# A decoder trunk's causal attention: heads kept in the rows of their product, and the causal mask as a VectorE add

## The chip, the core and the metric

One core of a Trainium2 chip runs the whole kernel in one launch. The metric is the device time of one execution in microseconds (us), as a median of several executions. A core has a matrix engine (TensorE, PE in the profile, with its weight loads as PEld), three other compute engines (VectorE = DVE, ScalarE = ACT, GpSimd = POOL), each with its own queue of instructions that it works off in order, and SyncE (SP), whose queue starts the transfers (DMAs). Matrix products land in PSUM, a small memory of banks; VectorE and ScalarE can read and write it, and everything else lies in SBUF, 128 partitions (rows) wide.

## What is computed

A trunk of two layers over 512 tokens of width 1024. In each layer four branches read the same input: RWKV-7 time mixing, multi-head latent attention, a convolution module and cross-attention into 256 memory tokens. Each branch is gated, projected and merged; an output product and a layer norm follow. The change is in the attention with latents (8 heads, 64 plain and 32 rotary channels each):

```python
q = (_rms_norm(q_lat, q_norm) @ w_uq).reshape(B, S, H, MLA_NOPE + MLA_ROPE)
kv = (_rms_norm(kv_lat, kv_norm) @ w_ukv).reshape(B, S, H, MLA_NOPE + MLA_V)
...
q_full = jnp.concatenate([q_nope, q_pe], axis=-1)
k_full = jnp.concatenate(
    [k_nope, jnp.broadcast_to(k_pe[:, :, None, :], (B, S, H, MLA_ROPE))], axis=-1)
...
s = jnp.einsum('bqhd,bkhd->bhqk', q_blk, k).astype(jnp.float32) * scale
s = jnp.where(key_idx[None, :] <= q_idx[:, None], s, MASK_VALUE)
pr = jax.nn.softmax(s, axis=-1).astype(v.dtype)
return jnp.einsum('bhqk,bkhd->bqhd', pr, v)
```

It is computed for blocks of 128 queries. Products are kept close to f32 precision: each operand is split into a high part in f32r (a shorter f32 for which TensorE is fast) and a low part, the rest, also in f32r.

## The kernel before

**A plan orders everything.** The program is written out while it is planned. Class `Plan` (line 67) keeps a clock for each engine and adds an estimated cost with each instruction; every branch is a generator that yields where something else may go first. `Plan.run` (147) steps the task that is due, or else takes the next piece of the stream of items (`stream`, 1860), which hold the large projections and serve as filler for TensorE. What results is a fixed order of instructions on each engine; no engine reorders its instructions at run time beyond that. All matrix products go through helper `MM` (line 286 of the profile), transposes through `TR` (291), vector and scalar work through `Engine` (235) and DMAs through `DMA` (298), so the profile shows these lines, and groups are told apart by the names of their tiles. All DMAs are issued from SP's one queue.

**Items and weights.** `stream` takes items in their listed order, skipping those that are not ready (`pick`, 1866). An item's weights are loaded as raw f32 (two buffers, `WR`), and split by ScalarE (high part) and VectorE (low part). A product of an item lands in one of the two banks of pool `pp`; the next one can use a bank when the instructions that read it are done.

**A product of split operands** is three matmuls (`mm3`, 467): high x low, high x high, low x high. 

**Pairs of heads.** `pair_item` (1416) computes queries ("pq") and keys ("pk") of two heads at once, 64 channels each, so that head 0 is on rows 0 to 63 of the product and head 1 on rows 64 to 127. `heads` (1441) splits the whole product into a high and a low tile ("xqh", "xql", "xkh", "xkl"), and eight DMAs for a pair copy the halves to rows 0 to 63 of each head's own tiles ("qT", "qTl", "kTh", "kTl"). The 32 rotary channels come to rows 64 to 95 by DMAs from "qrh", "qrl" (queries, in `pair_item`) and "krh", "krl" (keys, in `key_rotary`, 1299). The scores thus contract over 96 rows.

**Blocks.** `pair` (1454) spawns one `mla_block` (1471) for each head and each block of 128 queries, 64 in all over both layers, with up to three under way. A block is a chain across three engines: scores into a bank "ms" (three matmuls over 128 to 512 columns), the mask, row maximum on VectorE ("nmm"), exponential with row sum on ScalarE ("mP"), reciprocal and scaling on VectorE ("mP"), transposes on TensorE ("mt"), a copy on ScalarE ("mPT"), and for every two blocks of both heads the product with the values ("mo", 64 columns of weights). The mask is a fourth matmul into the diagonal 128 columns of "ms": the identity in bf16 as weights ("idb") times a tile with 0 and -1e30 ("causal").

**Around it.** The cross-attention ("xs", "xt", "xo") and the convolution run beside the causal attention. The convolution is 4 x 31 taps per layer on VectorE ("cacc", `taps`, 1123), each a pass over 128 x 512; after each it yields "slack", which lets the plan put it off until VectorE's clock. Its norm begins with transposes "ct". `mix` (682) makes the token shift of the RWKV branch in two passes: ScalarE scales the product, shifted by one column, into a tile "tsh", and VectorE adds the scaled product.

## Time and profile before

| | us |
|---|---|
| median of 3 executions | 1520.82 |
| lowest and highest | 1518.16, 1522.56 |
| the profiled execution, device time | 1519.87 |
| its span, first to last instruction | 1518.1 |
| first and last score matmul of layer 0 (from the span's start) | 121.5 and 223 |
| the same of layer 1 | 903 and 983 |

How to read the views: a window row gives a stretch of the span and for each engine its busy time and count of instructions. A wait row names the waiting engine and tile, after "<-" what ended the wait, then the sum in us, how many times, and the longest. A timeline row gives the start, the duration in us, the engine, line, operation, the tiles (out <- in), the shape and the count of merged instructions, and in brackets the idle time of the engine before it and what ended that. A group row ends with the busy time, the mean in ns of one, and the idle time before them. A matmul's duration covers its way through the array; matmuls overlap, so what one costs is read from the distance of the starts.

### The profile page before, as it was taken

What the parts mean: (1) busy time and instruction counts of PE and PEld (TensorE: products, weight loads), DVE (VectorE), ACT (ScalarE), POOL (GpSimd) and SP (SyncE); (2) the same over time, 40 slices, a digit from 0 to 9 for tenths busy, and PEclk for the clock granted to TensorE, in tenths of its full rate; (3) what the DMA queues carried; (4) which work ended last, traced back from release to release, by engine and by line L of the source; (5) the groups of instructions that cost most, each with busy time, mean ns of one, the idle gap of its engine ahead of it and who ended that gap; (6) DMA issues with size and microseconds to landing.
All of it is one profiled execution on the core that took longest, in us unless ns stands there. A gap on an engine that the chain in (4) does not pass through costs nothing.

```text
span 1518.1 us, 29700 instructions
## 1 busy us (share of the span) xinstructions
PE 1485.7 (98%) x11896; PEld 1238.0 (82%) x11896; DVE 1072.7 (71%) x2231; ACT 686.6 (45%) x1499; POOL 135.8 (9%) x323
## 2 busy tenths in 40 slices
PE   8999999999999999999999999999999999999997
PEld 8877788887887878888999877888887878788886
DVE  5788988765757675555554889997766586756747
ACT  5535653445245453344255556533443545443432
POOL 0000000030402021000010000000030303120002
PEclk9999999999999999999999999999999999999999
DMA  6443333322232323433343252433232323235231
GB/s 211 124 113 93 104 100 98 98 85 83 74 93 60 94 74 93 139 98 114 123 146 114 81 125 69 121 107 97 81 99 61 93 64 93 69 95 181 98 116 65
DMA packets 89018, 153.54 MB, mean 101 GB/s; under 512 B 41008, under 2 KB 47152, under 8 KB 88880
## 3 DMA queue, kind: packets, MB, share of 16 engines
q1 hardware_dynamic: 88880, 151.65, 33.9%
q8 instruction: 93, 1.52, 0.4%
q14 instruction: 45, 0.37, 0.1%
HBM read 134.32 MB, written 5.77 MB: 92 GB/s over the span
## 4 chain that ended last, share of the span: by engine, by line
PE 89%; DVE 5%; DMA 2%; ACT 2%; issue 1%; SPq 1%; POOL 0%; ACTq 0%; DVEq 0%; POOLq 0%
PE ps_m L286 22%; PE po L286 11%; PE ps_cg L286 3%; PE ps_rg L286 3%; PE ps_v L286 3%; PE ps_xg L286 3%; PE ps_mg L286 3%; PE ps_k L286 3%; PE ps_r L286 3%; PE ps_val L286 3%; PE pz L286 2%; PE ms L286 2%; PE pl L286 2%; PE ps_glu L286 2%; PE ps_xq L286 2%; PE x L286 2%
## 5 line engine op out<-in xcount | busy, mean ns | idle before, releaser
L235 DVE SCALAR_TENSOR_TENSOR cacc<-hpad,prm,cacc 128x512 f32<-128x512 f32 x240 | 178.9, 748 | 3.3
L235 ACT ACTIVATE tm<-ps_m,prm 128x512 f32<-128x512 f32 x64 | 44.1, 689 | 148.5 <-PE ps_m L286 134.7
L235 DVE SCALAR_TENSOR_TENSOR mt<-tm,po 128x512 f32<-128x512 f32 x48 | 33.0, 687 | 79.2 <-PE po L286 79.1
L235 POOL TENSOR_SCALAR ZT<-W 64x256 f32<-64x256 f32 x8 | 4.8, 600 | 621.8 <-DMA W<-scr 287.7
L235 POOL TENSOR_TENSOR ZT<-ZT,tmpW 64x14 f32<-64x14 f32 (+6 forms) x112 | 44.0, 393 | 8.8
L235 ACT ACTIVATE mP<-ms,nmm 128x512 f32<-128x512 f32 (+3 forms) x64 | 33.7, 529 | 18.3 <-DVE nmm L235 17.4
L235 POOL TENSOR_TENSOR tmpW<-ZT,W 64x14 f32<-64x14 f32 (+6 forms) x112 | 39.9, 356 | 7.9
L235 ACT COPY mPT<-mt 128x512 f32<-128x512 f32 (+3 forms) x64 | 26.7, 429 | 22.4 <-PE mt L291 17.1
L235 DVE TENSOR_TENSOR merged<-merged,mt 128x512 f32<-128x512 f32 x48 | 33.8, 704 | 1.6
L235 DVE TENSOR_REDUCE nmm<-ms 128x1 f32<-128x512 f32 (+3 forms) x64 | 29.9, 483 | 0.6 <-PE ms L286 0.2
L235 POOL TENSOR_SCALAR gr<-gm 128x8 f32<-128x8 f32 x8 | 2.3, 286 | 311.2 <-DVE gm L235 311.2
L291 PE MATMUL mt<-cst,mP 128*128 128x128 f32 x160 | 27.1, 276 | 2.6 <-DVE mP L235 2.2
L235 DVE SCALAR_TENSOR_TENSOR merged<-tm,po 128x512 f32<-128x512 f32 x16 | 11.0, 687 | 22.0 <-PE po L286 20.3
L235 DVE TENSOR_SCALAR mP<-mP,smm 128x512 f32<-128x512 f32 (+3 forms) x64 | 24.8, 387 | 2.3
L235 ACT ACTIVATE yb<-yb,mr,gr 128x64 f32<-128x64 f32 x64 | 22.1, 430 | 9.0 <-DVE mr L235 9.0
L235 POOL TENSOR_SCALAR lrs<-lmv 128x1 f32<-128x1 f32 x8 | 2.5, 315 | 263.5 <-DVE lmv L235 261.8
L291 PEld LDWEIGHTS mt<-cst,mP 128*128 128x128 f32 x160 | 18.6, 141 | 8.2 <-ACT mo L235 2.2
L235 ACT ACTIVATE z<-z,lnb,lrs 128x256 f32<-128x256 f32 (+1 forms) x16 | 9.6, 647 | 31.2 <-DVE lnb L235 31.2
L286 PE MATMUL ms<-kTl,qT 96*128 96x512 f32 (+3 forms) x64 | 22.2, 347 | 0.0
L286 PE MATMUL mo<-mPT,v 128*64 128x128 f32 x320 | 21.4, 278 | 0.5 <-ACT mPT L235 0.5
L286 PE MATMUL ms<-kTh,qT 96*128 96x512 f32 (+3 forms) x64 | 20.6, 322 | 0.0
L286 PEld LDWEIGHTS mo<-mPT,v 128*64 128x64 f32 x320 | 17.3, 136 | 4.0 <-issue 2.9
(3535 smaller groups left out, 5323.2 us busy)
## 6 DMA issues: line engine op xcount, KB each, us to landing
w<-in_w_ch_dram SPq DMA_DIRECT2D x146, 512.0 KB, 3.6
w<-in_w_o_dram SPq DMA_DIRECT2D x32, 512.0 KB, 3.6
w<-in_w_out_dram SPq DMA_DIRECT2D x16, 512.0 KB, 3.6
w<-in_w_lat_dram SPq DMA_DIRECT2D x16, 336.0 KB, 3.3
w<-in_w_mk_dram SPq DMA_DIRECT2D x8, 512.0 KB, 3.5
w<-in_w_mv_dram SPq DMA_DIRECT2D x8, 512.0 KB, 3.5
w<-in_w_qk_dram SPq DMA_DIRECT2D x8, 320.0 KB, 3.1
x<-in_xT_dram SPq DMA_DIRECT2D x8, 256.0 KB, 5.6
```

The source lines that it names most:

```text
L235: return self.plan.keep(f(*a, **k))
L286: plan.keep(nc.tensor.matmul(o, lhsT, rhs, start=start, stop=stop))
L291: plan.keep(nc.tensor.transpose(o, i, ident))
```

## The change

Heads keep the rows on which their product lands. Tiles of queries and keys get 128 rows. Head 0 of a pair has its plain channels on rows 0 to 63 and its rotary part on 64 to 95, as before, and contracts over rows 0 to 95. Head 1 has its plain channels on rows 64 to 127, its rotary part on rows 32 to 63 and zeros, set by GpSimd, on rows 0 to 31, and contracts over all 128. So `heads` splits each half of the product straight into the head's tiles, two instructions on ScalarE and two on VectorE in place of one and one, and the eight DMAs of a pair go. The mask matmul goes too; VectorE adds the tile "causal" to the diagonal 128 columns in PSUM ahead of the maximum.

Three changes of the order go with it: pair items are marked "apart" and are not picked right behind each other if another item is ready; taps yield "idle" and are due one step behind VectorE's clock; and `mix` no longer needs "tsh". With "idb" and "tsh" gone, the pool of general tiles has 33 slots, and one tile of the convolution moves to another pool.

```diff
-U_SLOTS = 32
+U_SLOTS = 33
...
-                elif task[2] == "slack":
-                    task[0] = max(task[0], self.clk["DVE"])
+                elif task[2] in ("slack", "idle"):
+                    task[0] = max(task[0], self.clk["DVE"] + (task[2] == "idle"))
...
         def mix(i, ps, dst):
-            S.activation(tsh[:, 1:512], ps[:, 0:511], AF.Copy, scale=pr("mu", i))
-            V.scalar_tensor_tensor(out=dst, in0=ps, scalar=PRM[l][2][:, i:i + 1], in1=tsh, op0=ALU.mult, op1=ALU.add)
+            S.activation(dst, ps, AF.Copy, scale=PRM[l][2][:, i:i + 1])
+            V.scalar_tensor_tensor(out=dst[:, 1:512], in0=ps[:, 0:511], scalar=pr("mu", i), in1=dst[:, 1:512], op0=ALU.mult, op1=ALU.add)
...
                 L["taps"][i] = k
-                yield "slack"
+                yield "idle"
...
-                t, z = u(f"ctn{i}" + t_), u(f"yc{i}" + t_)
+                t, z = sp.tile([128, 512], F32, tag="tg", name=f"ctn{i}" + t_), u(f"yc{i}" + t_)
...
-                    L["kT"] = [tuple(m(f"kT{n}{i}" + t_, 512, f"kT{n}{i}", 1, 96, F32R) for n in "hl") for i in range(4)]
+                    L["kT"] = [tuple(m(f"kT{n}{i}" + t_, 512, f"kT{n}{i}", 1, 128, F32R) for n in "hl") for i in range(4)]
+                    for i in (1, 3):
+                        for x in L["kT"][i]:
+                            G.memset(x[0:32].bitcast(F32), 0.0)
...
-            for kT in L["kT"]:
+            for i, kT in enumerate(L["kT"]):
                 for x, y in zip(kT, kr):
-                    DMA(x[64:96].bitcast(F32), y.bitcast(F32))
+                    DMA(x[ROPE[i % 2]].bitcast(F32), y.bitcast(F32))
...
+        ROPE, ROWS = [slice(64, 96), slice(32, 64)], [slice(0, 96), slice(0, 128)]
...
                     for x, y in zip(qT[h], qpe[hh // 2]):
-                        DMA(x[64:96].bitcast(F32), y[r:r + 32].bitcast(F32), f"qTpe{hh}{h}" + t_)
+                        if h:
+                            G.memset(x[0:32].bitcast(F32), 0.0)
+                        DMA(x[ROPE[h]].bitcast(F32), y[r:r + 32].bitcast(F32), f"qTpe{hh}{h}" + t_)
...
-        def heads(T, ps, n, s, there):
-
-            parts = [u(f"x{n}{x}" + t_, 512, F32R) for x in "hl"]
-            S.activation(parts[0], ps, AF.Copy, scale=s)
-            V.scalar_tensor_tensor(out=parts[1], in0=ps, scalar=s, in1=parts[0].bitcast(F32), op0=ALU.mult, op1=ALU.subtract)
-            plan.due(*parts)
-            yield
-            for i, x in enumerate(parts):
-                for h in range(2):
-                    y = T[h][i]
-                    DMA(y[0:64].bitcast(F32), x[HALF[h]].bitcast(F32), f"{n}{i}{h}" + y.tensor.name)
-                    there.append(f"{n}{i}{h}" + y.tensor.name)
+        def heads(T, ps, s, there):
+
+            for half, (hi, lo) in zip(HALF, T):
+                S.activation(hi[half], ps[half], AF.Copy, scale=s)
+                V.scalar_tensor_tensor(out=lo[half], in0=ps[half], scalar=s, in1=hi.bitcast(F32)[half], op0=ALU.mult, op1=ALU.subtract)
+                there.extend((hi, lo))
+                yield
...
-            mm3(ps, *(x[:, dg] for x in T[0]), *(x[:, 0:n] for x in T[1]), True, False)
-            MM(ps[:, dg], idb, causal, start=False, stop=True)
+            mm3(ps, *(x[ROWS[h], dg] for x in T[0]), *(x[ROWS[h], 0:n] for x in T[1]), True, True)
             yield
             P = m("mP" + q, 512, "mP", 3)[:, 0:n]
             nm, sm = st("nmm" + q, 1), st("smm" + q, 1)
+            V.tensor_tensor(out=ps[:, dg], in0=ps[:, dg], in1=causal, op=ALU.add)
             V.tensor_reduce(out=nm, in_=ps, axis=AX.X, op=ALU.max, negate=True)
...
         def pick():
+            second = None
...
                 if ready is None or ready():
-                    return n
+
+                    if not (apart and last[0]):
+                        return n
+                    second = n if second is None else second
+            if second is not None:
+                return second
```

More of the change, by code (lines that the diff above doesn't have):

```diff
@@ L1456, in pair @@
             mo, = yield from pg.take([128, 512], f"mo{hh}" + t_)
[L1457 removed]
+            plan.due(*there)
+            plan.t = max(plan.t, plan.done[f"qTpe{hh}1" + t_][0])
             yield
@@ L1863, in stream @@
         items, todo, held, runs = list(items), [], [], []
-        count, look = [0], [3]
+        count, look, last = [0], [3], [False]
         def pick():
-            for n, (blocks, run, ready, _, _) in enumerate(items):
+            second = None
+            for n, (blocks, run, ready, _, _, apart) in enumerate(items):
                 if not blocks and ready is None:
@@ L1884, in prefetch @@
                         return
-                    blocks, run, _, picked, _ = items.pop(n)
+                    blocks, run, _, picked, _, last[0] = items.pop(n)
                     if picked:
```

23 lines of the change are left out of this document (9 added, 14 removed).

## Prediction

> **What bounds the kernel now.** I read the page first: the busy shares, then the chain that ended last.
>
> ```profile
> span 1518.1 us, 29700 instructions
> PE 1485.7 (98%) x11896; PEld 1238.0 (82%) x11896; DVE 1072.7 (71%) x2231; ACT 686.6 (45%) x1499; POOL 135.8 (9%) x323
> PE 89%; DVE 5%; DMA 2%; ACT 2%; issue 1%; SPq 1%; POOL 0%; ACTq 0%; DVEq 0%; POOLq 0%
> ```
>
> TensorE is busy for 98% of the span and holds 89% of the chain, so time is gained by giving it less to do, or by ending the few waits it still has. A share over the whole span hides where those are, so next come the windows: lead-in, causal attention of layer 0, the rest of layer 0, causal attention of layer 1, the rest. Columns: stretch, its length, then busy time of PE, PEld, DVE, ACT, POOL.
>
> ```profile
> 0.00:100.00 100.00, 92.85 (x587) 86.66 (x588) 73.71 (x155) 54.26 (x118) 3.03 (x16) 1.00 0.48 151
> 100.00:235.00 135.00, 127.23 (x778) 102.37 (x777) 116.34 (x263) 72.37 (x192) 0.00 (x0) 0.99 0.41 105
> 235.00:860.00 625.00, 621.17 (x5235) 522.60 (x5234) 397.61 (x805) 273.07 (x566) 63.41 (x151) 1.00 0.33 98
> 860.00:990.00 130.00, 127.69 (x787) 103.76 (x787) 116.11 (x261) 75.03 (x192) 0.00 (x0) 1.00 0.38 100
> 990.00:1518.00 528.00, 516.73 (x4518) 422.63 (x4514) 368.89 (x752) 211.86 (x432) 69.38 (x156) 0.99 0.32 94
> ```
>
> The change works in the second and fourth stretch. There TensorE idles 7.8 us (135 - 127.23) and 2.3 us, and VectorE is nearly full: 18.7 and 13.9 us idle. What ended TensorE's longest waits in these two stretches (sum, times, longest; the first four rows are layer 0, the last is layer 1):
>
> ```profile
> PE pq L286 <- DVE xql L235: 2.8, 1, 2.8
> PE mt L291 <- DVE mP L235: 2.2, 2, 1.8
> PE ps_xq L286 <- DVE xql L235: 1.0, 1, 1.0
> PE xs L286 <- ACT xqh L235: 0.7, 1, 0.7
> ...
> PE xo L286 <- DVE xPTl L235: 2.0, 2, 1.6
> ```
>
> Together 8.7 us. The change can take time from two places only: TensorE's own work, and these waits.
>
> **1. The mask matmul goes (64 times).** Its price is not its duration but what it does to the spacing of starts. Layer 0, two score groups behind each other and the projection after them:
>
> ```profile
> 178.12 0.34 PE L286 MATMUL ms<-kTl,qT 96*128 96x384 f32 x1
> 178.30 0.33 PE L286 MATMUL ms<-kTh,qT 96*128 96x384 f32 x1
> 178.47 0.34 PE L286 MATMUL ms<-kTh,qTl 96*128 96x384 f32 x1
> 178.65 0.23 PE L286 MATMUL ms<-causal,idb 128*128 128x128 bf16 x1
> 178.69 0.42 PE L286 MATMUL ms<-kTl,qT 96*128 96x384 f32 x1
> 178.95 0.34 PE L286 MATMUL ms<-kTh,qT 96*128 96x384 f32 x1
> ```
>
> A 384-column product starts 0.18 us before the next one (178.12 to 178.30). The mask takes 0.04 (178.65 to 178.69), and the product after it 0.26 in place of 0.18: the step back from bf16 to f32r costs 0.08. So 0.12 where an f32r product follows. Where an f32 transpose follows, that step is paid later anyway:
>
> ```profile
> 157.42 0.23 PE L286 MATMUL ms<-causal,idb 128*128 128x128 bf16 x1
> 157.49 0.50 PE L291 MATMUL mt<-cst,mP 128*128 128x128 f32 x3
> ```
>
> 0.07 us. By the order of instructions of the program before, 41 of the 64 masks are followed by an f32r product, 18 by a transpose and 5 by the value matmul, which I count like the transposes: 41 x 0.12 + 23 x 0.07 = 6.5 us. In the order after, TensorE enters f32r from another type six times more often than before (220 against 214, masks left out): 6 x 0.08 = 0.5. Entries into 64-row tiles stay at 80, and outside the two stretches the order hardly moves. **TensorE's work: -6.0 us.** Bounds: 64 x 0.04 = 2.6 if only the mask's own step goes, 64 x 0.12 = 7.7. The odd head of a pair now streams through 128 rows in place of 96, as the projections do. Those pass a 512-column product in 0.23 us (the chain's own row, 24 of them):
>
> ```profile
> 236.30 5.44 PE ps_xg L286 x24
> ```
>
> By column that is no more than the 0.18 of 384 above, so nothing.
>
> [...]
>
> **2. The mask becomes a VectorE add (64 times), and the splits are done by halves.** The trace has no such add. Nearest are VectorE's 128-column pass over the same bank, and a split on 64 partitions beside those on 128:
>
> ```profile
> L235 DVE TENSOR_REDUCE nmm<-ms 128x1 f32<-128x128 f32 x16 | 4.2, 282 | 0.0
> L235 DVE SCALAR_TENSOR_TENSOR xql<-pq,xqh 128x512 fp32r<-128x512 f32 x8 | 5.5, 690 | 5.0 <-ACT xqh L235 4.7 <-DMA qTl<-xql 0.3
> L235 DVE TENSOR_TENSOR lxa<-lora,lxa 64x512 fp32r<-64x512 f32 x2 | 1.4, 690 | 0.0
> L235 ACT ACTIVATE xqh<-pq 128x512 fp32r<-128x512 f32 x8 | 4.8, 598 | 12.7 <-PE pq L286 12.7
> L235 DVE SCALAR_TENSOR_TENSOR cacc<-hpad,prm,cacc 128x512 f32<-128x512 f32 x240 | 178.9, 748 | 3.3
> ```
>
> I take 0.28 us for an add. Half the partitions cost as much as all (690 and 690), so the 16 splits of queries and keys become 32: 16 x 0.69 = 11.0 us more on VectorE and 16 x 0.60 = 9.6 on ScalarE. With the adds, VectorE gets 64 x 0.28 + 11.0 = 28.9 us more, 14.5 a layer, against 18.7 and 13.9 idle. That would just fill it. But the convolution's taps ("cacc") now step back for other work: by the order, 42 of them lie between the first and the last score of layer 0 before, 16 after; 35 and 22 in layer 1. That moves 39 x 0.75 = 29 us of VectorE work out, into stretches where it idles 227 and 159 us. So **nothing for the load**; without this cover the third rival sets in. Who waits for late taps is the convolution's norm. In the new order its first transpose stands 30 full products (7 us at 0.23) behind the last tap in layer 0, where it was 205, but in layer 1 only three and 65 small ones, where it was 77. If the taps run late there, that wait is new; I count nothing for it, since VectorE idles a third of that stretch.
>
> Each block's chain from score to probabilities is 0.28 longer. Up to three blocks are under way, with projections between their steps. Bounds: nothing, or 64 x 0.28 = 17.9 us. I take nothing: the row above has only 2.2 us of waiting for these probabilities today, with taps in the way:
>
> ```profile
> 146.30 1.53 DVE L235 SCALAR_TENSOR_TENSOR cacc<-hpad,prm,cacc 128x512 f32<-128x512 f32 x2
> 147.75 0.42 DVE L235 TENSOR_REDUCE nmm<-ms 128x1 f32<-128x256 f32 x1
> ```
>
> Two taps stood in front of the maximum that the next probabilities needed. With fewer taps there I take half of the 2.2 as gone: **-1.1**.
>
> **3. 64 copies between partitions go.** They are not on TensorE's path by themselves; they sit in SP's one queue, among the weight loads:
>
> ```profile
> qT<-xqh SPq DMA_DIRECT2D x16, 128.0 KB, 2.3
> ```
>
> Four such groups of 16, with 8 copies to a pair of heads. The waits at "ps_xq" (1.0) and "xs" (0.7) come from conversions that stand behind late weights or directly behind the product; in the new order the third pair has a value group between its key products, and the "xs" have other work in front. **-1.7**. Layer 1's "xo" wait of 2.0 I halve, since that order is redrawn too: **-1.0**. The copies of the rotary part stay, for odd heads with other target rows.
>
> **4. The first pair's wait stays, and grows.** This is the longest single one:
>
> ```profile
> 106.39 0.62 ACT L235 CAST w25h<-w 128x512 fp32r<-128x512 f32 x1 [1.90 <-DMA w<-in_w_ch_dram]
> 106.92 0.40 ACT L235 CAST w24h<-w 128x256 fp32r<-128x256 f32 x1
> 107.22 0.59 ACT L235 ACTIVATE xqh<-pq 128x512 fp32r<-128x512 f32 x1
> 107.84 0.69 DVE L235 SCALAR_TENSOR_TENSOR xql<-pq,xqh 128x512 fp32r<-128x512 f32 x1 [2.10 <-ACT xqh L235]
> 108.59 0.79 PE L286 MATMUL pq<-ltl,w24h 128*128 128x512 f32 x1 [2.78 <-DVE xql L235]
> 109.18 0.63 PE L286 MATMUL pq<-lth,w24h 128*128 128x512 f32 x1
> ...
> 111.74 0.45 PE L286 MATMUL pq<-lth,w24h 128*128 128x512 f32 x1
> ```
>
> ScalarE is in order: it waits for the weights w25, and behind that stands the split that frees the bank of "pq". After the wait the products are slow: from 108.59 to 111.74 seven of them take 3.15 us in place of 1.6, so 1.5 more. The new order has the same trap: the next product still needs that bank, ScalarE still casts a w25 (now the second pair's) ahead of the split, and the bank is free only after both halves. From 106.4: cast 0.4, half 0.5, cast 0.5, key half 0.5, half 0.5, then 0.69 on VectorE: 109.5, so **+1.0**. Every pair holds its bank some 0.6 us longer than before; besides this one, two pairs of layer 1 have nothing but their own six key products (1.4 us) between the query product and the next that needs the bank: **+1.2**. Bounds of this step: -4.3 (the weights land in time) and +1.0 + 8 x 0.69 = +6.5.
>
> **5. The rest.** 24 memsets on POOL, idle in both stretches:
>
> ```profile
> L235 POOL MEMSET reset<- 128x256 bf16 x1 | 0.3, 312 | 0.3 <-POOLq L2014 0.3
> ```
>
> Twice as many elements, an estimated 0.6 us each, long before the scores need them. The token shift ("mix") trades one ScalarE and one VectorE pass for one of each, of the same size. The 33rd slot and the moved tile only place data. Nothing.
>
> **Sum:** -6.0 - 1.1 - 1.7 - 1.0 + 1.0 + 1.2 = -7.6 us. The profiled execution took 1519.87 us for a span of 1518.1: 1512.3. The median before, 1520.82, is 0.95 above that execution, so I predict **1513 us**.
>
> **Rivals.** *The waits go too.* If the loads land in time without the 64 copies, all 8.7 us and the 1.5 of slow products may go: -6.0 - 10.2 = -16.2 at most, 1504.6. For it, a weight load that came late while the copies were in flight; against it, the first copy, issued when w25 was long late:
>
> ```profile
> ACT w26h L235 <- DMA w<-in_w_ch_dram: 4.0, 1, 4.0
> ...
> 107.84 1.15 SPq L298 DMA_DIRECT2D qT<-xqh  x2
> ```
>
> *The gain is eaten by banks.* Every pair, not three, holds its bank into the next product, and the other waits stay as they are: -6.0 + 6.5 = +0.5, 1521.3, no change. For it: pools of two banks, and halves split one after the other. Against: in the new order five of the eight pairs have other products in between. [...]
>
> *Slower: the add is paid on TensorE.* If projections run short between the blocks, each of the 64 chains shows its 0.28 us: +17.9 - 6.0 = +11.9, 1532.7. It decides where fewer than three steps of other work lie between a score and its transposes, so that TensorE reaches the transposes first. Against it: the order still puts projections between nearly all of them, and VectorE has fewer taps there.
>
> That the masks or copies stay is no rival: the order after has none of them.
>
> **How the numbers follow.** Forecast 0.61 (1509 to 1516), waits gone too 0.17, eaten 0.15, slower 0.07. A measurement of this kernel can tell about 0.3%, 4.6 us, from no change. The first two cases are faster: 0.78; same 0.15; slower 0.07. The range takes in the second and third case and leaves the slower one out: 1504 to 1522.
>
> **What would show it.** TensorE's idle time in the two stretches: about 9 us in place of 10.1. VectorE's "ms" adds at 0.28 us, 64 of them; fewer taps between scores. "ps_xq" waiting for "qTl" near 109 (step 4). Score groups followed by a product at its usual spacing, 0.18 for 384 columns, not 0.26 (step 1). The prediction is wrong if transposes of "mP" wait for VectorE in most blocks, if taps delay the convolution's norm, or if a "pq" bank is waited for at most pairs.

## The result, and the profile after

The changed kernel takes 1530.04 us (median of 4 executions, 1529.71 to 1531.98), the kernel before 1520.42 beside it: ratio 1.0066, interval [1.0049, 1.0084]. It is slower by 9.6 us (0.6%) where 1513 was forecast, in a range of 1504 to 1522. The profiled execution took 1529.76 us for a span of 1527.9.

The page of the changed kernel, busy times and the chain that ended last:

```profile
span 1527.9 us, 29615 instructions
PE 1487.9 (97%) x11832; PEld 1242.7 (81%) x11832; DVE 1104.5 (72%) x2310; ACT 696.8 (46%) x1515; POOL 150.7 (10%) x346
PE 91%; DVE 5%; ACT 2%; DMA 1%; issue 1%; POOL 0%; ACTq 0%; SPq 0%; DVEq 0%; POOLq 0%
```

TensorE has 64 instructions fewer (11896 before) and yet is busy 2.2 us longer. So idle time cannot be all of the loss; some matmuls must have become slower. The windows of the changed kernel (without the lead-in; stretch, length, busy time of PE, PEld, DVE, ACT, POOL, then granted clock, DMA share, GB/s):

```profile
...
100.00:235.00 135.00, 128.79 (x763) 105.60 (x762) 118.10 (x283) 79.47 (x204) 2.16 (x4) 0.97 0.24 73
235.00:860.00 625.00, 621.05 (x5246) 522.37 (x5245) 415.46 (x833) 273.65 (x569) 69.15 (x156) 1.00 0.32 98
860.00:990.00 130.00, 118.88 (x668) 97.38 (x667) 108.01 (x260) 71.26 (x183) 3.53 (x7) 0.93 0.21 63
990.00:1528.00 538.00, 525.25 (x4574) 429.99 (x4570) 388.87 (x784) 217.94 (x443) 69.00 (x156) 0.99 0.31 93
```

The fourth stretch, causal attention of layer 1, stands out. TensorE idles 11.1 us there (2.3 before), gets through 668 matmuls where it was 787, and the granted clock is 0.93 where it was 1.00; in layer 0 it fell from 0.99 to 0.97. What ended TensorE's waits in these two stretches, layer 0 first:

```profile
PE ps_xq L286 <- DVE qTl L235: 5.6, 2, 3.1
PE mo L286 <- ACT mPT L235: 0.5, 1, 0.5
```

```profile
PE ps_val L286 <- DVE qTl L235: 4.0, 1, 4.0
PE pq L286 <- DVE qTl L235: 3.9, 1, 3.9
PE ps_mg L286 <- DVE qTl L235: 2.2, 1, 2.2
PE ps_xq L286 <- DVE qTl L235: 0.9, 1, 0.9
```

All the waits of before that the prediction listed under "mP", "xs" and "xo" are gone. One kind has taken their place: six times, 16.6 us in all, a product that has nothing to do with the heads' low part waits for "qTl". It waits for the bank that this split still reads. One such pair of heads, the timeline of the changed kernel from the end of its query product (the six key products in between left out but for the last):

```profile
881.65 0.39 PE L286 MATMUL pq<-lth,w145l 128*128 128x512 f32 x1
...
882.08 0.59 ACT L235 ACTIVATE qT<-pq 64x512 fp32r<-64x512 f32 x1 [0.93 <-PE pq L286]
...
883.01 0.39 PE L286 MATMUL pk<-lth,w145l 128*128 128x512 f32 x1
883.02 0.61 ACT L235 CAST w147h<-w 128x512 fp32r<-128x512 f32 x1
883.27 0.68 DVE L235 SCALAR_TENSOR_TENSOR qTl<-pq,qT 64x512 fp32r<-64x512 f32 x1
883.53 0.62 ACT L235 CAST yxg0h<-xy 128x512 fp32r<-128x512 f32 x1
...
884.05 0.62 ACT L235 CAST w148h<-w 128x512 fp32r<-128x512 f32 x1
884.57 0.59 ACT L235 ACTIVATE kTh<-pk 64x512 fp32r<-64x512 f32 x1
885.19 0.59 ACT L235 ACTIVATE qT<-pq 64x512 fp32r<-64x512 f32 x1
...
886.51 0.69 DVE L235 SCALAR_TENSOR_TENSOR qTl<-pq,qT 64x512 fp32r<-64x512 f32 x1
...
887.35 0.76 PE L286 MATMUL pq<-ltl,w146h 128*128 128x512 f32 x1 [3.94 <-DVE qTl L235]
887.91 0.63 PE L286 MATMUL pq<-lth,w146h 128*128 128x512 f32 x1
```

The bank of "pq" has its product at 882.04 and is free at 887.20, 5.2 us later. The two halves are four steps in turn on two engines. Between the first half on ScalarE (882.08) and the second (885.19) stand a softmax step of the cross-attention (left out above), casts of weights, a cast for another branch and the keys' first half; ScalarE is never idle there. The key product is done at 883.40, the next product needs the bank of "pq", and TensorE stands still. Measured in this way, from the end of a product's last matmul to the end of the last split that reads its bank, the 16 products of the changed kernel hold their banks 77.4 us in all, 4.8 in the mean; before it was 34.1 and 2.1.

After the wait the matmuls start 0.43 us apart (887.91 and the next at 888.34) where 0.23 is usual, and the granted clock is 0.50 from 887.90 to 893.00. That stretch lies in the window row with 0.93, and it goes with TensorE being busy longer with fewer instructions.

### The profile page after: what moved, and what is told of

It reads as the page before. It is cut to its first block, busy times and chain, and to the rows that moved or that the text cites. A ratio compares the mean times of both kernels' runs of the same rounds, so it can differ in the third digit from the quotient of the medians.

```text
span 1527.9 us, 29615 instructions
## 1 busy us (share of the span) xinstructions
PE 1487.9 (97%) x11832; PEld 1242.7 (81%) x11832; DVE 1104.5 (72%) x2310; ACT 696.8 (46%) x1515; POOL 150.7 (10%) x346
## 4 chain that ended last, share of the span: by engine, by line
PE 91%; DVE 5%; ACT 2%; DMA 1%; issue 1%; POOL 0%; ACTq 0%; SPq 0%; DVEq 0%; POOLq 0%
PE ps_m L286 22%; PE po L286 11%; PE ps_mg L286 3%; PE ps_val L286 3%; PE ps_cg L286 3%; PE ps_rg L286 3%; PE ps_v L286 3%; PE ps_xg L286 3%; PE ps_xq L286 3%; PE ps_k L286 3%; PE ps_glu L286 3%; PE ps_r L286 3%; PE pz L286 2%; PE pl L286 2%; PE ms L286 2%; PE ps_mk L286 2%
## 5 line engine op out<-in xcount | busy, mean ns | idle before, releaser
L235 POOL TENSOR_TENSOR tmpW<-ZT,W 64x14 f32<-64x14 f32 (+6 forms) x112 | 43.1, 384 | 8.0
L291 PE MATMUL mt<-cst,mP 128*128 128x128 f32 x160 | 28.6, 281 | 0.1
L291 PEld LDWEIGHTS mt<-cst,mP 128*128 128x128 f32 x160 | 20.4, 144 | 6.8 <-issue 1.9
L235 DVE TENSOR_TENSOR ms<-ms,causal 128x128 f32<-128x128 f32 x64 | 18.7, 293 | 8.4 <-PE ms L286 8.2
L286 PE MATMUL ms<-kTl,qT 96*128 96x256 f32 (+4 forms) x64 | 21.8, 340 | 0.0
```

The costliest lines, as they stand in the source:

```text
L235: return self.plan.keep(f(*a, **k))
L286: plan.keep(nc.tensor.matmul(o, lhsT, rhs, start=start, stop=stop))
L291: plan.keep(nc.tensor.transpose(o, i, ident))
```

## The experiments

All ratios are against the kernel before, run beside each kernel. "Held" is the mean time that the 16 products of the pairs hold their banks, worked out from the timelines as above.

| run | what it is | median, us | ratio, interval | held, us |
|---|---|---|---|---|
| (before) | | 1520.4 | 1 | 2.1 |
| (changed) | | 1530.0 | 1.0066 [1.0049, 1.0084] | 4.8 |
| no_heads | change without the heads in place | 1509.6 | 0.9931 [0.9916, 0.9946] | 2.6 |
| heads_only | change without the mask on VectorE | 1535.5 | 1.0102 [1.0087, 1.0116] | 4.9 |
| sides_only | change without both | 1514.7 | 0.9961 [0.9948, 0.9975] | 2.1 |
| halves | before, splits in halves | 1538.9 | 1.0120 [1.0101, 1.0139] | 4.4 |
| one_go_q | changed, query halves in one go | 1526.3 | 1.0041 [1.0029, 1.0053] | 4.9 |
| free_first | changed, bank freed by a copy | 1529.7 | 1.0062 [1.0048, 1.0076] | 1.8 |
| apart_only | before, some side edits | 1513.4 | 0.9955 [0.9943, 0.9967] | 2.1 |
| idle_only | before, other side edits | 1512.9 | 0.9949 [0.9937, 0.9961] | 1.7 |
| twice_bank | no_heads, splits twice from the bank | 1544.7 | 1.0175 [1.0156, 1.0193] | 4.0 |
| twice_tile | no_heads, second time off the bank | 1519.9 | 1.0005 [0.9997, 1.0014] | 2.3 |
| mix_only | before, new mix | 1519.1 | 0.9997 [0.9988, 1.0005] | 2.1 |
| mask_best | no_heads, pairs not kept apart | 1515.3 | 0.9968 [0.9955, 0.9981] | 2.1 |
| same_no_heads | no_heads in the changed kernel's order | 1508.2 | 0.9918 [0.9904, 0.9931] | 2.2 |
| same_sides_only | sides_only in that order | 1512.6 | 0.9948 [0.9936, 0.9961] | 2.2 |
| same_free_first | free_first in that order | 1523.7 | 1.0019 [1.0010, 1.0028] | 1.8 |
| same_twice_tile | twice_tile in that order | 1515.2 | 0.9968 [0.9956, 0.9981] | 2.4 |
| same_twice_bank | twice_bank in that order | 1538.3 | 1.0122 [1.0103, 1.0141] | 4.7 |
| same_one_go | changed, all halves in one go, that order | 1522.1 | 1.0015 [1.0004, 1.0026] | 3.9 |

**Theory**: the heads in place cost the time, because the half steps hold a bank of the pool "pp" too long. **Rivals**: the 64 adds on VectorE; the new order of taps and items; splits that are late because their target tiles are still read by an earlier pair or being set to zero; the work of the added half steps as such. The expectations speak of 16.6 us of waits "in 8 places"; the wait rows above show six.

### The two parts apart

The kernel no_heads keeps everything but `heads`, `pair_item` and the tiles of queries and keys, which are those of before. The kernel heads_only keeps everything but this (and has the tile "idb" again, which the mask matmul needs):

```diff
-            mm3(ps, *(x[ROWS[h], dg] for x in T[0]), *(x[ROWS[h], 0:n] for x in T[1]), True, True)
+            mm3(ps, *(x[ROWS[h], dg] for x in T[0]), *(x[ROWS[h], 0:n] for x in T[1]), True, False)
+            MM(ps[:, dg], idb, causal, start=False, stop=True)
...
-            V.tensor_tensor(out=ps[:, dg], in0=ps[:, dg], in1=causal, op=ALU.add)
```

sides_only goes back on both and keeps the edits beside them (the tap rule, the rule for pairs, `mix`, the 33rd tile, the moved tile).

> All of the change but one part: a pair's product is split whole into two work tiles and copied head by head as before; the mask is added by VectorE, and the edits of the tap rule, the order of the items and the tiles stay. Theory (banks): the cost of the change is that queries and keys are split in four half steps in turn with other work, so that one of the two banks of the pp pool is held 4.8 us after a product in the mean of 16 and not 2.1, and the next product waits 16.6 us in 8 places. Then the waits go here, the 64 mask products are gone too, and the time is 1512 to 1517. Rival A (the 64 adds of 0.29 us on VectorE, 18.7 us in all, delay the splits and the scores): the time stays within 3 of the changed kernel's, 1527 to 1532. Rival B (the new order of taps and items costs it): also 1527 or more.

> All of the change but the other part: the mask is a product of identity and mask into the scores again, while queries and keys stay where their product leaves them. Theory (banks): the waits for the bank stay, and the mask's products come back, 64 at 0.07 to 0.12 us or some 6 us less what the adds cost: 1533 to 1539. Rival A (the adds on VectorE are the cost): without 18.7 us of adds on VectorE the time falls to 1520 to 1525. Rival B (order): 1529 or more, as with banks.

> Neither of the two parts: the kernel before with only the edits beside them, the tap rule that lets other VectorE steps go first, the rule that keeps two pairs apart in the stream, the mix without its shifted tile, one more work tile and the conv norm's tile in another pool. Theory (banks): 1518 to 1523, the time before. Rival B (the new order itself makes the changed kernel slow): 1527 or more.

Measured 1509.6, 1535.5 and 1514.7. With the heads in place the kernel is 20.4 us (1530.0 - 1509.6) or 20.8 us (1535.5 - 1514.7) slower, whichever way the mask is added; the mask on VectorE gives 5.1 or 5.5. So the adds are not the cost, and neither is the new order by itself: without both parts the kernel is faster than before. That last result, 1514.7, was expected by neither side, and 1509.6 lies below the theory's range.

### Halves without the new place

The kernel before, with the same work tiles and copies, but each product split by halves:

```diff
-            S.activation(parts[0], ps, AF.Copy, scale=s)
-            V.scalar_tensor_tensor(out=parts[1], in0=ps, scalar=s, in1=parts[0].bitcast(F32), op0=ALU.mult, op1=ALU.subtract)
-            plan.due(*parts)
-            yield
+            for half in HALF:
+                S.activation(parts[0][half], ps[half], AF.Copy, scale=s)
+                V.scalar_tensor_tensor(out=parts[1][half], in0=ps[half], scalar=s, in1=parts[0].bitcast(F32)[half], op0=ALU.mult, op1=ALU.subtract)
+                plan.due(*parts)
+                yield
```

> The kernel before with one edit: each product of a pair is split in two halves of 64 partitions, with other steps between them, into the same work tiles as before, and copied from there as before; the mask is a product as before. Theory (banks held by four half steps): the banks are held as long as in the changed kernel, and the time goes up by 5 to 12 us, 1525 to 1532. Rival C (the halves are late because they are written straight into tiles whose earlier readers, the scores of an earlier pair, or whose memset on GpSimd must be done first): nothing waits on such a tile here, and the time is that of before, 1518 to 1523.

1538.9, 19 us above before and more than the theory said. The waits for a bank come back under other names (here "xql" is the low part that reads "pq"):

```profile
PE pq L286 <- DVE xql L235: 9.2, 3, 4.8
...
PE ps_xq L286 <- DVE xql L235: 4.0, 2, 2.8
PE ps_mg L286 <- DVE xql L235: 3.2, 1, 3.2
PE ps_glu L286 <- DVE xql L235: 3.2, 1, 3.2
```

Nothing is written straight into a head's tile here, so the place of writing is out. Held bank and added work are still one.

### Shorter holding, more work

The changed kernel with the query's four half steps issued in one go (one_go_q; only the queries have a scale other than 1), and with a whole copy first that frees the bank (free_first):

```diff
                 there.extend((hi, lo))
-                yield
+                if s == 1.0:
+                    yield
```

```diff
+            x = u("raw" + T[0][0].tensor.name)
+            S.activation(x, ps, AF.Copy, scale=s)
+            yield
             for half, (hi, lo) in zip(HALF, T):
-                S.activation(hi[half], ps[half], AF.Copy, scale=s)
-                V.scalar_tensor_tensor(out=lo[half], in0=ps[half], scalar=s, in1=hi.bitcast(F32)[half], op0=ALU.mult, op1=ALU.subtract)
+                S.activation(hi[half], x[half], AF.Copy)
+                V.tensor_tensor(out=lo[half], in0=x[half], in1=hi.bitcast(F32)[half], op=ALU.subtract)
```

> The changed kernel with one edit: the four half steps of the queries (two on ScalarE, two on VectorE) are issued in one go, with no other step between them; those of the keys are still in turn with other work. Theory (the bank of the queries is held too long because other steps stand between the halves): the bank is free some 2.0 us after its product at best (0.59 + 2 x 0.69 and the hand-overs) and not 4.4; the products that waited 16.6 us in 8 places wait a third of that, and the time is 1516 to 1522. Rival (the work of 16 more half steps on each of the two engines is the cost, not the time the bank is held): the work is the same, 1527 to 1531.

> The changed kernel with one edit: a pair's product is first copied whole, scaled, into a work tile by one ScalarE instruction of some 0.6 us, which frees its bank, and the halves are split from that tile, straight into the heads' tiles, in four half steps in turn with other work as in the changed kernel. It is 16 ScalarE instructions more than the changed kernel, some 9.5 us. Theory (banks): the waits for the bank go although the halves and their place stay, and the time is 1508 to 1516. Rival (the work of the half steps is the cost): with still more work 1530 to 1540. Rival (writing straight into the heads' tiles is the cost): 1527 or more.

1526.3 and 1529.7. Both miss the theory. In one_go_q the theory's step hardly happened: the queries hold their banks 4.1 us in the mean, where it was 4.4 and the theory had 2.0, and the keys 5.8, where it was 5.3. In free_first the theory's step happened and its result did not: held falls to 1.8, no product waits for "qTl" any more, and the time stays. Alone it would fit the rival of the place of writing, against which halves stands. One thing had moved that was not in the edit. By the instructions of the program, 989 full products of 512 columns stand between the first query product of layer 1 and the start of its second recurrence (the serial part of the RWKV branch), where the changed kernel has 872; the recurrence then has fewer products beside it, and its matmuls wait. By the table of stretches below its attentions are as fast as those of no_heads, and what it loses lies behind them. The plan writes the order from its own estimates, so each edit draws a new one.

### The same work on and off the bank

no_heads, each product split twice, with other steps between. In twice_bank both times read the bank (first diff); in twice_tile the second time reads and rewrites the work tiles (second diff):

```diff
-            S.activation(parts[0], ps, AF.Copy, scale=s)
-            V.scalar_tensor_tensor(out=parts[1], in0=ps, scalar=s, in1=parts[0].bitcast(F32), op0=ALU.mult, op1=ALU.subtract)
-            plan.due(*parts)
-            yield
+            for _ in range(2):
+                S.activation(parts[0], ps, AF.Copy, scale=s)
+                V.scalar_tensor_tensor(out=parts[1], in0=ps, scalar=s, in1=parts[0].bitcast(F32), op0=ALU.mult, op1=ALU.subtract)
+                plan.due(*parts)
+                yield
```

```diff
+            S.activation(parts[0], parts[0].bitcast(F32), AF.Copy)
+            V.scalar_tensor_tensor(out=parts[1], in0=parts[1].bitcast(F32), scalar=0.0, in1=parts[1].bitcast(F32), op0=ALU.mult, op1=ALU.add)
+            plan.due(*parts)
+            yield
```

> All of the change but the heads in place (1509.6 us as it stands, splits whole and copied), with one edit: each product of a pair is split twice, whole, into the same two work tiles, both times read from its bank, with other steps between. That is 16 more ScalarE instructions of 0.59 us and 16 more VectorE instructions of 0.69, as many as the halves add, and the bank is held until the second time is done. Theory (what costs is that the bank is held): as with the halves, 1522 to 1532. Rival (what costs is the work of 16 more steps on each engine): also 1520 or more, but then as much with the second time read from the work tiles, in the run beside this one.

> As the run beside this one, but the second time reads and rewrites the work tiles: as many more instructions of the same size, none of which touches the bank, which is free after the first. The copies into the heads' tiles start later by the second time. Theory (the bank): 1508 to 1515, the time of the kernel without them (1509.6) but for a little. Rival (the work): as much as in the run beside this one, 1520 or more.

1544.7 and 1519.9: the bank makes 25 us of difference at equal work, but the kernel with the work off the bank is also 10 slower than no_heads where nearly nothing was expected. Here too the order had moved (941 and 938 products ahead of the second recurrence), so the 10 us cannot be put down to the work yet.

### The side edits, and the order's own share

apart_only is sides_only with the old tap rule (first diff); idle_only is sides_only, and mask_best is no_heads, without the rule for pairs (second); mix_only is the kernel before with the new `mix` alone (third):

```diff
                 L["taps"][i] = k
-                yield "idle"
+                yield "slack"
```

```diff
-                 lambda: ... and MEM[l] is not None, apart=True)
+                 lambda: ... and MEM[l] is not None)
```

```diff
-            S.activation(tsh[:, 1:512], ps[:, 0:511], AF.Copy, scale=pr("mu", i))
-            V.scalar_tensor_tensor(out=dst, in0=ps, scalar=PRM[l][2][:, i:i + 1], in1=tsh, op0=ALU.mult, op1=ALU.add)
+            S.activation(dst, ps, AF.Copy, scale=PRM[l][2][:, i:i + 1])
+            V.scalar_tensor_tensor(out=dst[:, 1:512], in0=ps[:, 0:511], scalar=pr("mu", i), in1=dst[:, 1:512], op0=ALU.mult, op1=ALU.add)
```

> The kernel before with some of the edits beside the two parts: two pairs kept apart in the stream, the mix without its shifted tile, one more work tile and the conv norm's tile in another pool; the taps keep their old rule. The kernel with these and the new tap rule took 1514.7, the kernel before 1519.9. Theory (the two pairs that follow each other directly wait for their bank, 3.2 us at 105 us of the kernel before, and the order takes that away): 1514 to 1517 here. Rival (the tap rule gives the 5 us): 1518 to 1522.

> The kernel before with the new tap rule, the mix without its shifted tile, one more work tile and the conv norm's tile in another pool; pairs may follow each other directly as before. Theory (the order of the pairs gives the 5 us): 1518 to 1522. Rival (the tap rule gives it, since the splits and softmax steps no longer queue behind taps of 0.75 us): 1514 to 1517.

> The kernel before with one edit: the mix without its shifted tile (ScalarE scales the product into the result, VectorE adds the shifted product to it). Two kernels with this, one more work tile, another pool for the conv norm's tile and one of two edits of the order took 1513.4 and 1512.9, before 1519.9 to 1520.4. Theory (the one shifted tile ties 26 mixes to each other, and that was worth some 5 us): 1513 to 1517. Rival (the gain is the order that comes out with one work tile more): 1518 to 1522.

> The candidate to beat both kernels: the mask on VectorE, splits whole and copied as before, the new tap rule, the mix without its shifted tile, one more work tile and the conv norm's tile in another pool, but pairs not kept apart. With the pairs kept apart it took 1509.6. Theory (the mask is worth 5 us wherever the splits leave the bank early, and without it this order took 1512.9): 1506 to 1509. Rival (what the mask gave was that order's luck): 1510 to 1514.

apart_only keeps the rule for pairs, idle_only that for taps, and both keep the mix, the 33rd tile and the moved tile: 1513.4 and 1512.9, so neither rule alone is needed for the gain. The mix alone gives nothing (1519.1). What is left is the 33rd tile with the moved tile, or the order that comes out with them; that is not settled. mask_best, no_heads without the rule for pairs, took 1515.3, slower than no_heads and than idle_only: by this pair the mask on VectorE loses 2.4 us. At this size a comparison of two kernels with different orders says little.

### One order for all

So the order in which the changed kernel's stream takes its items was written out as a list and given to the others; every kernel here has 866 or 872 products ahead of the second recurrence. The list fixes the items alone. Where the small steps stand between them, those of the recurrence too, the plan still decides.

```diff
         def pick():
-            second = None
...
+            for n, (_, run, ready, _, soon, *_) in enumerate(items):
+                if place[id(run)] == PICKS[-len(items)]:
+                    return n if ready is None or ready() or soon and soon() else None
             return None
```

same_one_go has this edit beside it:

```diff
             for half, (hi, lo) in zip(HALF, T):
                 S.activation(hi[half], ps[half], AF.Copy, scale=s)
+            for half, (hi, lo) in zip(HALF, T):
                 V.scalar_tensor_tensor(out=lo[half], in0=ps[half], scalar=s, in1=hi.bitcast(F32)[half], op0=ALU.mult, op1=ALU.subtract)
                 there.extend((hi, lo))
-                yield
+            yield
```

> The kernel with the mask on VectorE and whole, copied splits (1509.6 in its own order), its items taken in the very order of the changed kernel (1530.0). Theory (the bank held by the half steps costs some 20 us, the order little): 1507 to 1514. Rival (the difference of 20 us is in good part the order that each kernel happened to get): 1518 or more.

> The kernel with neither part (1514.7 in its own order) in the order of the changed kernel. Against the run beside this one it gives what the mask on VectorE is worth when nothing else moves. Theory (the 64 mask products cost TensorE 5 to 6 us and the adds are hidden): 4 to 7 above that run, 1513 to 1519. Rival (the adds are paid in part, and the three pairs so far, -5.1, -5.4 and +2.4, were the order's): 0 to 3 above it, or below it.

> The changed kernel with a whole copy of the product that frees its bank, then the halves from the copy (1529.7 in its own order, in which 989 large products stood before the second recurrence of layer 1), in the order of the changed kernel (872). Theory (held banks are the cost, and the gain was lost in the last stage by the order): 1508 to 1517. Rival (the half steps themselves and the added copy cost as much as the held bank): 1525 or more.

> The kernel whose splits are done twice, the second time from the work tiles with the bank free (1519.9 in its own order, with 938 large products before the second recurrence of layer 1), in the order of the changed kernel (872). Theory (16 more steps on each engine cost nothing while the bank is free, and the 10 us were the order's): 1508 to 1514, within 3 of the kernel without the second time. Rival (the work costs the 10 us): 1517 or more.

> The kernel whose whole splits are done twice from the bank (1544.7 in its own order, with 941 large products before the second recurrence of layer 1), in the order of the changed kernel. The kernel beside it with the second time off the bank took 1515.2 in that order. Theory (the held bank is the greater part of the cost, at equal work): 1527 to 1538, that is 12 to 23 more. Rival (the work is the cost, and the 25 us between the two in their own orders were the order's): 1515 to 1521.

> The changed kernel with the half steps of queries and of keys issued in one go, the two of ScalarE, then the two of VectorE, with no other step between them, in the order of the changed kernel. The queries alone in one go gave 1526.3. Theory (turn taking makes the holding long: 4.8 us where 2.0 to 2.7 would do): 1515 to 1521. Rival (four steps at full price hold the bank whatever stands between, and load the engines as much): 1524 to 1530.

same_no_heads takes 1508.2: with the items in one order the heads in place cost 21.8 us (1530.0 - 1508.2). It beats both kernels by 12 and 22 us. Its windows of the two attentions:

```profile
100.00:235.00 135.00, 130.69 (x788) 108.62 (x787) 120.38 (x287) 77.52 (x201) 0.00 (x0) 1.00 0.40 108
860.00:990.00 130.00, 128.58 (x764) 105.77 (x763) 117.37 (x271) 72.30 (x185) 0.00 (x0) 1.00 0.40 110
```

TensorE idles 5.7 us in place of the changed kernel's 17.3, and the clock is 1.00 in both. same_sides_only takes 1512.6, so the mask on VectorE gives 4.5 us in that order, within the theory's 4 to 7.

The pair that has equal work: 1515.2 off the bank, 1538.3 from it. The held bank costs 23.1 us at equal work and with the items in one order. Waits of the one on the bank:

```profile
PE ps_xq L286 <- DVE xql L235: 6.3, 3, 3.6
...
PE ps_mg L286 <- DVE xql L235: 6.0, 2, 3.1
PE pq L286 <- DVE xql L235: 3.7, 1, 3.7
PE ps_xg L286 <- DVE xql L235: 3.6, 1, 3.6
PE ps_val L286 <- DVE xql L235: 2.0, 1, 2.0
```

Together 21.6 us; off the bank the same names have 3.7. same_twice_tile is 7.0 above same_no_heads (1515.2 - 1508.2), between the theory's "within 3" and the rival's 9 or more. The waits that grew in same_twice_tile are mostly in the recurrence and in the softmax:

```profile
PE x L286 <- DVE PT L235: 3.9, 5, 1.8
PE mt L291 <- DVE mP L235: 2.9, 2, 2.6
...
PE bo L286 <- DVE cn L235: 2.0, 1, 2.0
```

In same_no_heads the first two are 1.1 and 0.7, and the third is absent.

same_one_go issues both ScalarE halves and then both VectorE halves without other steps between; 1522.1, a little above the theory's end. Held falls from 4.8 to 3.9 only, and the waits for "qTl" and "kTl" from 16.6 to 9.8 us. Without the turn taking 8 of the 22 us are gone from the time, and more from the attentions, as the table below shows. same_free_first, 1523.7, fits neither side: the bank's waits are gone (0.8 us is left), but the softmax now waits, and the recurrence too:

```profile
PE mt L291 <- DVE mP L235: 4.0, 4, 2.2
PE ty L291 <- ACT yb L235: 3.1, 4, 2.3
PE x L286 <- DVE PT L235: 3.0, 3, 1.7
...
PE ps_xq L286 <- ACT rawqT L235: 0.8, 1, 0.8
```

Here are 16 more ScalarE copies, and the heads are ready later.

Where the time of these kernels goes is seen by stretches. In the profiled execution of each, take the distance between the starts of two matmuls that follow each other, and from it the median of such pairs (same shapes, same output tiles) over all 20 profiles; the sum of what is left is the loss. "Attentions" are the two stretches from the first query product of a layer to its recurrence, "outside" is all else. The recurrence runs in four steps; the last column counts the full products between the first query product of layer 1 and the last of these steps.

| run | span, us | loss in the attentions, us | loss outside, us | products |
|---|---|---|---|---|
| (before) | 1518.1 | 37.8 | 71.4 | 1622 |
| (changed) | 1527.9 | 51.9 | 71.7 | 1622 |
| same_no_heads | 1503.9 | 30.1 | 69.5 | 1622 |
| same_twice_bank | 1538.6 | 61.0 | 71.9 | 1622 |
| same_twice_tile | 1515.4 | 32.4 | 77.4 | 1598 |
| same_one_go | 1521.3 | 36.9 | 79.5 | 1598 |
| same_free_first | 1522.1 | 37.0 | 80.3 | 1670 |
| no_heads | 1508.5 | 31.5 | 71.6 | 1622 |
| twice_tile | 1519.5 | 28.5 | 84.4 | 1685 |
| twice_bank | 1549.0 | 56.6 | 85.6 | 1685 |
| free_first | 1526.2 | 29.9 | 82.9 | 1760 |

In the attentions the bank decides, with the items in one order as in each kernel's own. Splits done twice from the bank lose 28.6 and 28.1 us more there than splits done twice off it, and the added work off the bank loses next to nothing (32.4 against 30.1 in the one order, 28.5 against 31.5 in their own). The changed kernel loses 21.8 more than same_no_heads; with all halves in one go it is 6.8 more, with the bank freed first 6.9, and free_first in its own order loses no more than no_heads.

The rest is lost outside. That loss is 69.5 to 73.0 us in all 13 profiles with 1622 products and 77.4 to 85.6 in the six with 1598 or with 1670 and more (one_go_q, with 1640, has 70.9). With 1598 it is the second recurrence itself that loses more (33.0 and 33.7 us, against 27.0 to 29.2 in the 13). With 1670 and more it is also what follows its last matmul (9.8 to 12.9 us against 3.7 to 4.8), where less filler is left. So the loss outside goes with how the plan spreads the filler and not with the added steps, of which same_twice_bank has as many as same_twice_tile. This is read across the runs; no run changes the spread alone. Whether a third bank in "pp" would do better was not tried.

## Why the prediction was wrong

The difference of 9.6 us parts, with the items in the changed kernel's order, into -7.8 (1520.4 to 1512.6, side edits and order), -4.5 (mask) and +21.8 (heads in place).

**The step that failed is 4**, "Every pair holds its bank some 0.6 us longer than before", priced at +1.2 beside the first pair's +1.0. Three things were wrong in it. First, the size: 2.7 us longer, not 0.6. I added the durations of the second half and took for granted that the halves follow each other. But `heads` yields between them, and the plan puts casts, keys and other branches there, each in order on the same two engines. Second, who waits: I counted a pair as safe if other products stand between it and the next pair. Those products use the same two banks; the waits above are at "ps_xq", "ps_val" and "ps_mg". What counts is only the product after the keys, whichever it is. Six of eight pairs waited, which is one of the three signs by which the prediction called itself wrong; TensorE's idle time in the two stretches is 17.3 us and not about 9. Third, the price of a wait: by the table above 21.8 of the 24.0 us between the two profiled spans (1527.9 and 1503.9) lie in the attentions. Waits for a bank make 14.6 of them (16.6 us, and 2.0 in same_no_heads), and full products at the slow pace some 7 (35 of them start over 0.36 us before the next, 2 in same_no_heads); what else changed there, waits for the softmax and other distances, cancels within 0.3. The prediction had the slow matmuls at its first wait, 1.5 us, and gave none to the others. That first pair's wait did stay, at "ps_xq" near 108 as foretold, and grew from 2.78 to 3.09 us, so by 0.3 and not 1.0.

The rival "The gain is eaten by banks" named the mechanism and got 1521.3, because it used the same 0.69 us a pair. The upper end of step 4's own bounds, +6.5, was no bound: it assumed the shortest holding.

**Step 1** holds as far as one pair of kernels can tell. With the items in one order the kernel without mask matmuls is 4.5 us faster in the median and 6.2 in the spans of the profiled executions (1510.1 and 1503.9); -6.0 was predicted, bounds -2.6 and -7.7. **Step 2**: an add takes 0.293 us (0.28 estimated), and half the partitions do cost as much as all (687 ns on VectorE and 592 on ScalarE for 64 rows, where 128 rows took 690 and 598 in the kernel before):

```profile
L235 DVE TENSOR_TENSOR ms<-ms,causal 128x128 f32<-128x128 f32 x64 | 18.7, 293 | 8.4 <-PE ms L286 8.2
L235 DVE SCALAR_TENSOR_TENSOR qTl<-pq,qT 64x512 fp32r<-64x512 f32 x16 | 11.0, 687 | 3.6 <-ACT qT L235 3.1
L235 ACT ACTIVATE qT<-pq 64x512 fp32r<-64x512 f32 x16 | 9.5, 592 | 8.9 <-PE pq L286 8.0 <-DVE smx L235 0.8
```

That the adds are hidden, at least for the most part, was right: paid in full they would have cost 17.9 us, and the mask part gains 4.5. That 16 more steps on each engine cost nothing as load fits the attentions of the two kernels that do them off the bank (2.3 us more and 3.0 less). What they cost in the changed kernel, they cost by holding the bank. The -1.1 for the softmax wait was not earned by the mask: in same_no_heads transposes wait 3.4 us for the probabilities,

```profile
PE mt L291 <- DVE smm L235: 2.2, 1, 2.2
...
PE mt L291 <- DVE mP L235: 0.7, 1, 0.7
...
PE mt L291 <- ACT mP L235: 0.5, 1, 0.5
```

and the kernel with mask matmuls in the same order has no such wait. **Step 3**: the "xs" and "xo" waits went, but they are gone in same_sides_only too, which keeps all 64 copies. So it was not the going of the copies that ended these waits, and no run shows a gain from it. The wait at "ps_xq" did not go but became the bank's. **Step 5**, "Nothing" for mix, slot and tile: 7.8 us with the order that comes with them, and not from the mix alone (1519.1). In the first attention same_sides_only has

```profile
100.00:235.00 135.00, 133.26 (x816) 108.48 (x815) 120.22 (x269) 73.71 (x197) 0.00 (x0) 1.00 0.40 109
```

1.7 us idle in place of 7.8.

The kernel takes the two banks of "pp" in turn, so that one is emptied while the next product runs. The trace shows where that ends: with six key matmuls (1.4 us) between, a bank held 5.2 us (882.04 to 887.20) left TensorE waiting for 3.94 us.

## What to carry to other kernels

Price an edit of the instructions that empty a PSUM bank by how long the bank is held, to the end of the last reader and with everything that may be queued between, against the time until the next product that needs any bank of that pool. Where a scheduler writes the order, a yield inside such a step is part of its price, and two kernels are compared by a few us only in one order, written out; even then the small steps move, so the stretch that an edit works in is compared first, and the whole time second. Splitting one full-width pass into two half-width passes buys no time per pass here (687 against 690 ns on VectorE, 592 against 598 on ScalarE); it only lengthens the chain (banks held 4.8 us in the mean, and 2.1 before).

## What was not expected of the hardware

Slow matmuls behind a wait of 2.2 us, in the changed kernel:

```profile
944.57 0.39 PE L286 MATMUL pk<-lth,w151l 128*128 128x512 f32 x1
947.17 0.47 PE L286 MATMUL ps_mg<-xl,w152h 128*128 128x512 f32 x1 [2.21 <-DVE qTl L235]
947.48 0.39 PE L286 MATMUL ps_mg<-xh,w152h 128*128 128x512 f32 x1
947.71 0.53 PE L286 MATMUL ps_mg<-xh,w152l 128*128 128x512 f32 x1
948.04 0.63 PE L286 MATMUL ps_mg<-xl,w152h 128*128 128x512 f32 x1
...
951.35 0.39 PE L286 MATMUL ps_mg<-xh,w152l 128*128 128x512 f32 x1
```

The first three start 0.31, 0.23 and 0.33 us ahead of the next, near the usual 0.23; then the distance is 0.43 us until 951.02, and 0.23 again from 951.35. So the slow stretch begins 0.9 us after the wait has ended and lasts some 3.3 us, 1.5 us lost on top of 2.2; the granted clock is 0.52 from 948.04 to 951.35 and 1.00 from there to 960. Behind the wait of 0.9 us (layer 1, "ps_xq") no distance of 0.43 follows; behind the 3.94 us at 887.35 it lasts until about 893.

The length of the wait does not settle it. In same_one_go two waits of 2.28 us for the bank, with the granted clock of the 8 us behind each:

```profile
107.81 0.47 PE L286 MATMUL ps_xq<-xl,w24h 128*128 128x512 f32 x1 [2.28 <-DVE qTl L235]
954.99 0.47 PE L286 MATMUL ps_val<-xl,w154h 128*128 128x512 f32 x1 [2.28 <-DVE qTl L235]
108.00:116.00 8.00, 8.00 (x44) 6.73 (x44) 7.56 (x21) 3.80 (x13) 0.00 (x0) 1.00 0.53 162
955.00:963.00 8.00, 8.00 (x42) 6.17 (x43) 6.83 (x15) 2.96 (x8) 0.00 (x0) 0.79 0.38 132
```

The first is followed by matmuls at the usual pace, the second by a slow stretch. The wait of 1.56 us at "xo" in layer 1 is followed by matmuls at the usual pace in the kernel before, whose granted clock is 1.00 from 860 to 1010; in mix_only, which has that wait too, the clock of that stretch is 0.99. What decides between the two cases is not shown. Behind the 2.78 us ahead of the slow products that the prediction shows, the granted clock was 0.50 (108.59 to 111.74).
